# Long convolutions by FFT: 128x128 transpositions on TensorE instead of shuffles by DMA

## The chip, the cores and the metric

The kernel runs on one core of a Trainium2 chip. The metric is the time of one execution on the device in microseconds (us). Of the kernel before, three timed runs gave 4006.89, 4009.58 and 4015.99 us; their median is 4009.58 us.

## What is computed

The reference is a pair of transformer-like blocks, each a token mixer and a mixture of experts. The change touches the mixer of the first block alone, a Hyena operator on 1024 tokens of 1024 channels: two long convolutions, each gated, with filters as long as the sequence on both sides.

```python
def long_conv(zin, o):
    zf = zin.astype(F32)
    y = jnp.fft.irfft(jnp.fft.rfft(zf, n=2 * L, axis=1) * kf[None, :, o], n=2 * L, axis=1)[:, :L]
    return (y + zf * f_bias[o].astype(F32)).astype(h.dtype)
z = x1 * long_conv(v, 0)
z = x2 * long_conv(z, 1)
return z @ w_out + b_out
```

`L` is 1024, so the transforms have length 2048. `kf` are the spectra of the filters, which the kernel computes beforehand.

## The kernel before

The program runs in stages. First come the filters' spectra (`filters`), the input's norm and the input projection, woven together. Then comes `gamma`, all the long convolutions. After it `hyena_out` projects the result, and the experts, the second block and its experts follow. `gamma` is the stage of the change.

A transform of 2048 is done in two steps, over 128 x 16. A token is n = 16 n1 + n2. A stage of products over n1 turns 64 values of n1 (the other 64 are the zero padding) into 128 rows of sines and cosines; a second one, over n2 and a group of 8 rows, gives the spectrum, in 16 blocks. Between the two, what stood on partitions as (row of 8, block) with n2 along the free side must stand as (n2, row of 8) on partitions with the block along the free side. The inverse has the same two stages in reverse. All data are float32; a float32 product is two records of TensorE in the trace.

`convs` is one stream: two quarters of the channels (256 each), for each quarter both convolutions. Two streams run. For each convolution a stream does the following, and the shared pool `fft2` with five buffers of 128 x 16 x 256 (`shuf`) holds A, B, Y, C and E of both streams:

- *First stage* (L424): for each of 8 steps two products of 128 columns by 256, over all 128 partitions of `z`. Partitions 0 to 63 and 64 to 127 hold two different n2, so the table `f1z` has zeros for the half that is not meant. ScalarE copies the PSUM bank (tag `c1`, named `c` in the trace) to A (L425).
- *Shuffle* (L282, called for each n2): SyncE issues a DMA from A to B, 128 KB from all partitions to 8 partitions. 16 for a convolution.
- *Spectrum* (L292, `spectrum`): for each of 8 steps four 128 x 64 products by 256, of which two write partitions 0 to 63 and two 64 to 127. `consume` multiplies by the filter's spectrum, with VectorE (L437, L438), and adds up on VectorE and GpSimd (L448, L449) into Y.
- *Third stage* (L459): the inverse of the second, 16 products by 256, copied by ScalarE to C (L460); then 16 shuffles from C to E (L462).
- *Last stage* (L472): 16 products of 128 x 64 into tag `tp`; for the first convolution VectorE multiplies by the gate into `z` (L475), for the second ScalarE copies to `zt`, TensorE transposes (L485), VectorE multiplies by the gate (L487), and the result `zc` goes to DRAM.

The filter's spectra `kl`, the gate and the next `z` are loaded by SyncE too, so they stand in the same queue as the shuffles. PSUM has 3 banks of `c1`, 2 of `tp` and 3 of `ri`. Which stream's step is written next is set in `gamma` by a table `GP` of rests; the framework's scheduler then orders each engine's instructions by its own model.

Of the kernel before, what the change touches and what calls it, by code (L numbers as in the profile page):

```python
# [23 lines left out]
OP = mybir.AluOpType  # L24
# [14 lines left out]
def host_consts():  # L39
    """Tables that depend on shapes alone."""  # L40
# [23 lines left out]
    # by place in a block of 8, then block  # L64
# [37 lines left out]
    c["g2i"] = Gi.reshape(128, 2048)  # L102
# [25 lines left out]
    # t > j, t <= i, t < j, t >= i: in chunks of 64, then in one of 128  # L128
# [9 lines left out]
    # rows (segment, expert): same expert, and earlier segment of it  # L138
# [5 lines left out]
def bcast(ap, n, off=0, parts=128):  # L144
    """Row of a DRAM tensor on every partition."""
    return bass.AP(tensor=ap.tensor, offset=ap.offset + off, ap=[[0, parts], [1, n]])


def turn_pair(ap):
    """[p, 2, n] with the two swapped."""  # L150
    a = [list(x) for x in ap.ap]
    return bass.AP(tensor=ap.tensor, offset=ap.offset + a[-2][0], ap=[*a[:-2], [-a[-2][0], 2], a[-1]])


def turned(ap):
    """[..., n] with the last in reverse."""
# [4 lines left out]
def weave(*gens):  # L161
    """Emits generators in turn: (generator, yields, from, to) over a span of 1."""
# [8 lines left out]
def part(g, n):  # L171
    """The next n steps of a generator."""
# [4 lines left out]


GP = (1.0, 1.0, 0, 0, 8)


class Kern:
# [17 lines left out]
    def behind(self, *marks):  # L200
        """What is traced here is issued after these, engine by engine."""
# [10 lines left out]
    sep = "tp"  # tag of transposes  # L212
# [4 lines left out]
    # ------------------------------------------------------------------ hyena  # L217
    def hyena_tables(self, pool, inv):
# [4 lines left out]
        else:  # L223
            self.f1z = self.load(pool, "f1z", [128, 2, 128], I["k_f1z"].rearrange("p (h m) -> p h m", h=2))
# [72 lines left out]
    def filters(self, ctx):  # L297
        """Spectra of the two filters, normalised, with the bias as a tap at zero, to DRAM."""
# [26 lines left out]
        def taps(o, q):  # L325
# [4 lines left out]
            for n2 in range(16):  # L330
# [6 lines left out]
                # sum of the positive taps: with that of all taps, it gives the sum of their sizes  # L337
# [11 lines left out]
        def out(o, q, B, acc):  # L349
# [41 lines left out]
    def convs(self, i, qs, wk, wk2):  # L391
        """Both long convolutions of quarters of the channels, gated, tokens in (n2, n1) order: from xg[0]
        by tokens to zc by channels. A step is a bank of products; a shuffle follows steps 8 and 24 of the 32."""
        nc, CW = self.nc, self.CW
        own = lambda name, shape, p=wk: p.tile([128, *shape], F32, name=f"{name}{i}", bufs=1)
        shuf = lambda: self.fft.tile([128, 16, CW], F32, name="shuf")

# [21 lines left out]
        for n, (q, o) in enumerate([(q, o) for q in qs for o in range(2)]):  # L419
            A, B = shuf(), shuf()  # L420
            for j in range(8):
                pa = self.pt(self.ps, "c1", [2, CW])
                for h in range(2):
                    nc.tensor.matmul(pa[:, h, :], lhsT=self.f1z[:, h, :], rhs=z[:, j, :], start=(h == 0), stop=(h == 1), skip_group_check=True)  # L424
                nc.scalar.copy(A[:, 2 * j:2 * j + 2, :], pa)  # L425
                for h in range(2):
                    self.shuffle(A, B, 2 * j + h)
                if j == 7:
                    g = gates(o, q)
                yield  # L430
            Y = shuf()
# [1931 lines left out]
```

## Time and profile before

| what | value |
|---|---|
| median of 3 runs | 4009.58 us (4006.89 to 4015.99) |
| profiled execution, first to last instruction | 4012.2 us |
| TensorE busy, whole span | 3334.1 us (83%) |
| VectorE busy | 2680.1 us (67%) |
| ScalarE busy | 1914.8 us (48%) |
| GpSimd busy | 894.5 us (22%) |
| stage of the long convolutions | 678.3 to 1176 us |

The profiled execution's own time is the span; it lies among the times of the three runs. The stage is 12% of it. Busy times of TensorE count a product's whole passage through the array, so that neighbours overlap: the time from start to start is what a product costs in a row of products.

### The profile page before, as it was taken

To read this page: it belongs to the slowest core of one execution; us is meant where nothing else is said; L and a number is where in the kernel's file an instruction comes from. 1 tells how busy PE (TensorE), PEld (TensorE's weight loads), DVE (VectorE), ACT (ScalarE), POOL (GpSimd) and SP (SyncE) were. 2 spreads that over 40 slices of the span, in tenths; PEclk is the share of its full clock that TensorE was granted. 3 is DMA by queue.
4 is the path that set the end of the run, shared out by engine and by line. 5 is a ranking of instruction groups with operands and counts; after the bars stand their busy time and mean duration, and the time that the engine had idled before them with its cause. 6 is when DMAs were issued, how large, how long until landed. Compare 5 with 4: busy or idle time off the path is not lost. (4 is left out here: it accounts for less than half of the span.)

```text
span 4012.2 us, 48518 instructions
## 1 busy us (share of the span) xinstructions
PE 3334.1 (83%) x17602; PEld 2631.6 (66%) x17602; DVE 2680.1 (67%) x3397; ACT 1914.8 (48%) x2511; POOL 894.5 (22%) x829
## 2 busy tenths in 40 slices
PE   4699998455649699999999999779987898895996
PEld 2466666333337578877777777567877797783775
DVE  5443442432439778888888888767538886757987
ACT  5433332111124356666666666566424443333665
POOL 1111110221216501020001000020136444423331
PEclk8899999777879799999999999989998998896998
DMA  8667674776774699999999999746543435427998
GB/s 230 103 169 168 152 197 141 132 145 114 152 168 125 204 338 367 357 348 363 361 351 368 358 368 352 247 146 196 159 154 97 120 104 151 158 95 260 370 359 307
DMA packets 558959, 908.43 MB, mean 226 GB/s; under 512 B 88696, under 2 KB 291039, under 8 KB 555615
## 3 DMA queue, kind: packets, MB, share of 16 engines
q1 hardware_dynamic: 542608, 852.42, 68.0%
q0 software_dynamic: 11312, 43.26, 3.9%
q10 hardware_dynamic: 4800, 9.64, 0.7%
q8 instruction: 140, 2.29, 0.2%
q14 instruction: 99, 0.81, 0.1%
HBM read 735.40 MB, written 119.48 MB: 213 GB/s over the span
## 5 line engine op out<-in xcount | busy, mean ns | idle before, releaser
L518 DVE TENSOR_TENSOR wl<-raw,wh 128x2048 fp32r<-128x2048 f32 x474 | 1067.1, 2286 | 114.4 <-ACT wh L517 113.4
L517 ACT CAST wh<-raw 128x2048 fp32r<-128x2048 f32 x480 | 889.2, 1907 | 80.8 <-PE ab L526 36.9
L525 PE MATMUL ab<-wl,xT 128*128 128x512 f32 x1280 | 515.4, 403 | 37.4 <-DVE wl L518 37.4
L524 PE MATMUL ab<-wh,xT 128*128 128x512 f32 x1280 | 511.4, 402 | 1.1 <-ACT wh L517 1.1
L526 PE MATMUL ab<-wh,xT 128*128 128x512 f32 x1280 | 510.8, 399 | 0.0
L525 PEld LDWEIGHTS ab<-wl,xT 128*128 128x128 f32 x1280 | 243.7, 190 | 106.0 <-DVE wl L518 52.1
L524 PEld LDWEIGHTS ab<-wh,xT 128*128 128x128 f32 x1280 | 243.5, 190 | 59.0 <-ACT wh L517 3.3
L526 PEld LDWEIGHTS ab<-wh,xT 128*128 128x128 f32 x1280 | 243.1, 190 | 54.4
L525 PE MATMUL y<-wl,hT 128*128 128x512 f32 x640 | 257.0, 402 | 0.2 <-DVE wl L518 0.2
L292 PE MATMUL ri<-shuf,g2f 128*64 128x256 f32 x1024 | 154.5, 430 | 122.9 <-DMA shuf<-shuf 115.7
L1078 POOL DMA_INDIRECT xe<-hl,idx x32 | 52.2, 1631 | 908.1 <-DVE idx L1076 810.0
L524 PE MATMUL y<-wh,hT 128*128 128x512 f32 x640 | 253.1, 396 | 1.5 <-DVE ye L1157 1.5
L526 PE MATMUL y<-wh,hT 128*128 128x512 f32 x640 | 252.9, 395 | 0.0
L292 PEld LDWEIGHTS ri<-shuf,g2f 128*64 128x64 f32 x1024 | 77.3, 152 | 187.3 <-issue 133.1
L525 PE MATMUL u<-h2T,pwh 128*128 128x512 f32 (+1 forms) x400 | 161.1, 404 | 3.3 <-DVE h2T L518 3.3
L1166 POOL DMA_INDIRECT acc<-ye,idx x30 | 106.0, 3533 | 255.3 <-DVE ye L1157 221.8
L526 PE MATMUL u<-h2T,pwl 128*128 128x512 f32 (+1 forms) x400 | 160.6, 403 | 0.0
L517 ACT CAST hT<-tp 128x512 fp32r<-128x512 f32 x80 | 46.9, 586 | 235.8 <-PE tp L1109 235.8
L524 PE MATMUL u<-hT,uwh 128*128 128x512 f32 x384 | 158.5, 413 | 1.1 <-ACT ub L701 0.9
L524 PE MATMUL u<-h2T,pwh 128*128 128x512 f32 (+1 forms) x400 | 157.5, 402 | 0.0
L437 DVE TENSOR_TENSOR t<-ri,kl 128x512 f32<-128x512 f32 x64 | 43.9, 686 | 167.1 <-PE ri L292 89.1
L525 PE MATMUL u<-hT,uwh 128*128 128x512 f32 x384 | 155.3, 404 | 0.0
(548 smaller groups left out, 7196.5 us busy)
## 6 DMA issues: line engine op xcount, KB each, us to landing
raw<-in_moe_w_dram SPq DMA_DIRECT2D x384, 1024.0 KB
shuf<-shuf SPq DMA_DIRECT2D x384, 128.0 KB
raw<-in_exp_w_gate_dram SPq DMA_DIRECT2D x32, 1024.0 KB
raw<-in_exp_w_up_dram SPq DMA_DIRECT2D x32, 1024.0 KB
raw<-in_exp_w_down_dram SPq DMA_DIRECT2D x32, 1024.0 KB
pwl<-in_w_in_dram SPq DMA_DIRECT2D x37, 512.0 KB
gw<-in_mod_w_dram SPq DMA_DIRECT2D x32, 512.0 KB
kf<-kst SPq DMA_DIRECT2D x32, 512.0 KB
```

The costliest lines, as they stand in the source:

```text
L292: nc.tensor.matmul(ri[s * 64:s * 64 + 64, t, :], lhsT=self.g2f[:, 2 * qq + s, o:o + 64], rhs=B[:, 2 * qq + s, :], start=(t == 0), stop=(t ...
L437: nc.vector.tensor_tensor(t1[0][:, h], ri, k, op=OP.mult)
L517: c = self.nc.scalar.copy(hi, src)
L518: (eng or self.nc.vector).tensor_tensor(lo, src, hi, op=OP.subtract)
L524: nc.tensor.matmul(pt, lhsT=l[0], rhs=r[0], start=first, stop=False)
L525: nc.tensor.matmul(pt, lhsT=l[0], rhs=r[1], start=False, stop=False)
L526: nc.tensor.matmul(pt, lhsT=l[1], rhs=r[0], start=False, stop=last)
L1078: nc.gpsimd.indirect_dma_start(out=xe, out_offset=None, in_=hlD, in_offset=bass.IndirectOffsetOnAxis(ap=idx[:, 0:1], axis=0))
L1166: nc.gpsimd.indirect_dma_start(out=accD, out_offset=row, in_=ye, in_offset=None, compute_op=OP.add)
```

## The change

A and C are now made with the channels on partitions: the data `z` and Y are the stationary side of the product and the tables the moving one. A 128 x 128 transposition on TensorE for each block (or n2) and half of the channels then brings the rows back to partitions, and ScalarE or VectorE copies it out of PSUM to B or E. The first stage's table has no zeros any more: a product takes the 64 partitions of one n2 alone, the other half's product goes to another PSUM bank and another half of the array's rows. Its copies write runs of 8 elements into A. The third stage's products write PSUM in runs of 8 elements with gaps (`pa[:, c, :, s, :]`). The order of steps in `convs` changes: the transpositions of the next step are written before the spectrum products of this one, and the third stage's products inside the spectrum's loop, two steps behind. Two steps of the last stage share a bank of tag `ri` in place of one of `tp` each. The next `z` is loaded at the end of the second convolution's first stage. `GP` is gone: the streams are woven at an offset of half a convolution. Comments are gone in the whole file, so line numbers differ. The shuffles in `filters` stay.

```diff
-    fz = np.zeros((128, 2, 128))
-    fz[:64, 0] = F1t[:64]
-    fz[64:, 1] = F1t[:64]
-    c["f1z"] = fz.reshape(128, 256)
+    c["f1n"] = np.concatenate([F1[:64], F1[:64]])
...
-    c["g2i"] = Gi.reshape(128, 2048)
+    c["g2i"] = Gi.reshape(128, 16, 8, 16).transpose(0, 1, 3, 2).reshape(128, 2048)
...
-            A, B = shuf(), shuf()
-            for j in range(8):
-                pa = self.pt(self.ps, "c1", [2, CW])
+            A = shuf()
+            Av = chans(A)
+            for j, c in ((0, 0), (0, 1), (4, 0), (4, 1)):
+                pa = [self.pt(self.ps, "c1", [4, 128]) for _ in range(2)]
+                for m in range(4):
+                    for h in range(2):
+                        r = slice(h * 64, h * 64 + 64)
+                        nc.tensor.matmul(pa[h][:, m, :], lhsT=z[r, j + m, c * 128:c * 128 + 128], rhs=self.f1n[r, :],
+                                         start=(m == 0), stop=(m == 3), tile_position=(h * 64, 0), skip_group_check=True)
                 for h in range(2):
-                    nc.tensor.matmul(pa[:, h, :], lhsT=self.f1z[:, h, :], rhs=z[:, j, :], start=(h == 0), stop=(h == 1), skip_group_check=True)
-                nc.scalar.copy(A[:, 2 * j:2 * j + 2, :], pa)
-                for h in range(2):
-                    self.shuffle(A, B, 2 * j + h)
-                if j == 7:
+                    nc.scalar.copy(Av[:, c].rearrange("p b (n k) -> p n b k", k=8)[:, 2 * j + h:2 * j + h + 7:2], pa[h].rearrange("p n (b k) -> p n b k", k=8))
+                if j and c:
                     g = gates(o, q)
+                    if o == 1 and q != qs[-1]:
+                        z = first(qs[qs.index(q) + 1])
                 yield
-            Y = shuf()
+            B, Y = shuf(), shuf()
+            def turn(qq):
+                pt = self.pt(self.ps, "tp", [2, CW])
+                for s in range(2):
+                    for c in range(2):
+                        b = 2 * qq + s
+                        nc.tensor.transpose(pt[:, s, c * 128:c * 128 + 128], Av[:, c, b, :], self.ident)
+                nc.scalar.copy(B[:, 2 * qq:2 * qq + 2, :], pt)
...
-            yield from self.spectrum(B, consume)
-            C, E = shuf(), shuf()
-            for b in range(8):
-                pa = self.pt(self.ps, "c1", [2, CW])
-                for h in range(2):
-                    nc.tensor.matmul(pa[:, h, :], lhsT=self.g2i[:, 2 * b + h, :], rhs=Y[:, 2 * b + h, :], start=(h == 0), stop=(h == 1), skip_group_check=True)
-                nc.scalar.copy(C[:, 2 * b:2 * b + 2, :], pa)
-                for h in range(2):
-                    nc.sync.dma_start(E[16 * b + 8 * h:16 * b + 8 * h + 8], C[:, 2 * b + h, :])
+            def back(b):
+                if b == 0:
+                    C.append(shuf())
+                pa = self.pt(self.ps, "c1", [2, 16, 2, 8])
+                for s in range(2):
+                    for c in range(2):
+                        nc.tensor.matmul(pa[:, c, :, s, :], lhsT=Y[:, 2 * b + s, c * 128:c * 128 + 128], rhs=self.g2i[:, 2 * b + s, :],
+                                         start=(s == 0 and c == 0), stop=(s == 1 and c == 1), skip_group_check=True)
+                nc.scalar.copy(chans(C[0])[:, :, :, 16 * b:16 * b + 16], pa.rearrange("p c n s k -> p c n (s k)"))
+            C = []
+            sp = self.spectrum(B, consume)
+            turn(0)
+            for qq in range(8):
+                if qq < 7:
+                    turn(qq + 1)
+                next(sp)
+                if qq % 2 and qq > 1:
+                    back(qq - 3)
+                    back(qq - 2)
...
-            for j in range(8):
-                pa = self.pt(self.ps, "tp", [CW])
+            for j in range(0, 8, 2):
+                for k in (j, j + 1):
+                    pt = self.pt(self.ps, "tp", [2, CW])
+                    for h in range(2):
+                        for c in range(2):
+                            nc.tensor.transpose(pt[:, h, c * 128:c * 128 + 128], Cv[:, c, 2 * k + h, :], self.ident)
+                    if k % 2:
+                        nc.vector.tensor_copy(E[:, 2 * k:2 * k + 2, :], pt)
+                    else:
+                        nc.scalar.copy(E[:, 2 * k:2 * k + 2, :], pt)
+                pa = self.pt(self.ps, "ri", [2, CW])
...
+        weave(*[(self.convs(i, (i, i + 2), wk, wk2), 4 * 18 + 1, i * 9 / 81, (72 + i * 9) / 81) for i in range(2)])
```

First place: TensorE's order in the first stage of the second quarter's convolutions, before. L424 is the first stage, L472 the last stage, `c_...` the PSUM bank.

```order
L424 MATMUL c_5900<-z_5755,f1z 128x256 x2
L472 MATMUL tp<-shuf,if_5058 64x256 x4
L424 MATMUL c_5910<-z_5755,f1z 128x256 x2
L424 MATMUL c_5920<-z_5755,f1z 128x256 x2
L424 MATMUL c_5942<-z_5755,f1z 128x256 x2
L472 MATMUL tp<-shuf,if_5058 64x256 x4
```

The same place now. L427 is the first stage (two banks for the two halves), L443 the transposition to B, L288 the spectrum, L474 the third stage.

```order
L443 MATMUL tp<-ident,shuf 128x128 x4
L474 MATMUL c_6796<-g2i,shuf 128x16x8 x4
L427 MATMUL c_6802<-f1n,z_5588 128x128 x4
L288 MATMUL ri<-shuf,g2f 64x256 x4
L427 MATMUL c_6803<-f1n,z_5588 128x128 x4
L288 MATMUL ri<-shuf,g2f 64x256 x3
L427 MATMUL c_6829<-f1n,z_5588 128x128 x2
L427 MATMUL c_6830<-f1n,z_5588 128x128 x2
```

Two products of 256 columns a bank have become four of 128 columns a bank, and the two halves of a pair (c_6802 and c_6803) stand apart, with the other stream's spectrum between.

Second place: TensorE's order in the middle of a spectrum, before. L292 is the spectrum, L459 the third stage.

```order
L459 MATMUL c_5275<-shuf,g2i 128x256 x2
L292 MATMUL ri<-shuf,g2f 64x256 x8
L459 MATMUL c_5292<-shuf,g2i 128x256
L459 MATMUL c_5307<-shuf,g2i 128x256
L292 MATMUL ri<-shuf,g2f 64x256 x4
L459 MATMUL c_5292<-shuf,g2i 128x256
```

The same place now. L504 is the transposition to E, L512 the last stage of the other stream.

```order
L443 MATMUL tp<-ident,shuf 128x128 x4
L288 MATMUL ri<-shuf,g2f 64x256 x4
L504 MATMUL tp<-ident,shuf 128x128 x8
L512 MATMUL ri<-shuf,if_5178 64x256 x2
L443 MATMUL tp<-ident,shuf 128x128 x4
L288 MATMUL ri<-shuf,g2f 64x256 x4
L512 MATMUL ri<-shuf,if_5178 64x256 x2
L504 MATMUL tp<-ident,shuf 128x128 x8
L474 MATMUL c_7006<-g2i,shuf 128x16x8 x4
```

Each spectrum step now has its transpositions in front of it, and the other stream's last stage stands between them with its own.

Third place: SyncE's queue around the first spectra, before. `kl`, `gate` and `z` are loads, the two lines of `shuf<-shuf` in question are L282 and L462.

```order
L282 DMA shuf<-shuf 8x16x256 x2
L412 DMA gate_5189<-xg_72 128x8x256
L406 DMA kl_0_5313<-kf 128x2048
L462 DMA shuf<-shuf 8x16x256 x8
L406 DMA kl_0_5314<-kf 128x2048
L462 DMA shuf<-shuf 8x16x256 x4
L406 DMA kl_1_5410<-kf 128x2048
```

The same place now.

```order
L411 DMA gate_5283<-xg_72 128x8x256
L192 DMA if_5178<-in_k_if_dram 128x64
L405 DMA kl_0_5249<-kf 128x2048
L405 DMA kl_0_5250<-kf 128x2048
L405 DMA kl_1_5570<-kf 128x2048
```

The loads stand one behind the other, with no shuffle between.

## Rows read from the trace of the kernel before

**Rows 1.** Windows: each stretch with its length, busy time by engine, clock, DMA.
```profile
core 0: us, PE busy (x) PEld busy (x) DVE busy (x) ACT busy (x) POOL busy (x), PEclk, DMA share, GB/s
678.30:1176.00 497.70, 263.25 (x1344) 165.97 (x1344) 166.20 (x240) 86.07 (x162) 110.61 (x80) 0.76 0.72 137
...
1040.00:1100.00 60.00, 45.13 (x232) 26.84 (x231) 23.72 (x41) 13.74 (x24) 13.85 (x10) 0.88 0.65 155
```

**Rows 2.** Waits, 665 to 1180 us: engine, line, releaser, total us, times, longest.
```profile
PE ri L292 <- DMA shuf<-shuf: 97.5, 6, 29.4
...
PE tp L472 <- DMA shuf<-shuf: 89.0, 7, 21.8
...
PE tp L472 <- DMA ld<-in_hy_w_out_dram: 28.6, 1, 28.6
...
PE ri L292 <- DVE t L438: 5.7, 4, 3.2
```

**Rows 3.** DMA in the stage: queue (packets, MB, share), issues.
```profile
q1 hardware_dynamic: 47251, 67.81, 71.8%
...
shuf<-shuf SPq DMA_DIRECT2D x256, 128.0 KB
```

**Rows 4.** Timeline at the stage's end: start, length, instruction, idle time before and releaser.
```profile
1166.97 3.57 PE L472 MATMUL tp<-shuf,if 128*64 128x256 f32 x16 [28.61 <-DMA ld<-in_hy_w_out_dram]
...
1184.21 0.79 PE L524 MATMUL u<-Wo,zT 128*128 128x512 f32 x1 [6.51 <-DMA zr<-zc]
```

**Rows 5.** Timeline of TensorE in a dense stretch of a spectrum.
```profile
758.77 1.95 PE L292 MATMUL ri<-shuf,g2f 128*64 128x256 f32 x16
...
766.87 1.13 PE L459 MATMUL c<-shuf,g2i 128*128 128x256 f32 x4
...
767.93 1.08 PE L292 MATMUL ri<-shuf,g2f 128*64 128x256 f32 x8
...
768.95 1.99 PE L459 MATMUL c<-shuf,g2i 128*128 128x256 f32 x8
```

**Rows 6.** Timeline of TensorE: eight transpositions and what follows them.
```profile
907.57 1.04 PE L485 MATMUL tp<-ident,zt 128*128 128x128 f32 x8
908.45 1.03 PE L459 MATMUL c<-shuf,g2i 128*128 128x256 f32 x4
```

**Rows 7.** Timeline of TensorE in the delta rule: 128x128 products, then others.
```profile
3200.35 2.05 PE L1784 MATMUL g<-R,w 128*128 128x128 f32 x16 [0.17 <-DVE qT L1711]
3202.15 0.36 PE L1716 MATMUL g<-cmask,idr 128*128 128x256 f32 x1
```

**Rows 8.** Groups by line in the stage: busy us, mean ns, idle before.
```profile
L437 DVE TENSOR_TENSOR t<-ri,kl 128x512 f32<-128x512 f32 x64 | 43.9, 686 | 167.1 <-PE ri L292 89.1 <-issue 77.1
...
L425 ACT COPY shuf<-c 128x512 f32<-128x512 f32 x64 | 37.3, 586 | 113.7 <-PE c L424 89.0 <-DMA shuf<-shuf 24.7
...
L475 DVE TENSOR_TENSOR z<-tp,gate 128x256 f32<-128x256 f32 x32 | 13.6, 425 | 89.0 <-PE tp L472 87.7 <-PE ri L292 1.2
```

**Rows 9.** Groups by line, whole span: two ScalarE copies of one size.
```profile
L1400 ACT COPY pub<-u 128x512 f32<-128x512 f32 x18 | 18.9, 1061 | 2.7 <-PE u L526 2.7
...
L1459 ACT COPY pub<-u 128x512 f32<-128x512 f32 x14 | 8.2, 584 | 14.3 <-PE u L526 14.3
```

**Rows 10.** Windows of the delta rule, columns as in rows 1.
```profile
3060.00:3120.00 60.00, 52.09 (x411) 50.51 (x411) 48.89 (x123) 29.75 (x82) 30.23 (x32) 0.93 0.32 86
3120.00:3180.00 60.00, 49.60 (x397) 46.58 (x397) 53.65 (x113) 27.84 (x83) 31.21 (x37) 0.95 0.45 131
3180.00:3240.00 60.00, 54.79 (x434) 53.15 (x434) 51.66 (x123) 30.89 (x93) 27.81 (x32) 0.91 0.40 113
3240.00:3300.00 60.00, 55.09 (x467) 52.55 (x465) 48.13 (x131) 27.70 (x78) 18.85 (x23) 1.00 0.40 108
```

More of the change, by code (lines that the diff above doesn't have):

```diff
@@ L176, in part @@
         yield
-GP = (1.0, 1.0, 0, 0, 8)
 class Kern:
@@ L223, in hyena_tables @@
         else:
-            self.f1z = self.load(pool, "f1z", [128, 2, 128], I["k_f1z"].rearrange("p (h m) -> p h m", h=2))
+            self.f1n = self.load(pool, "f1n", [128, 128], I["k_f1n"])
             self.g2i = self.load(pool, "g2i", [128, 16, 128], I["k_g2i"].rearrange("p (b m) -> p b m", b=16))
@@ L396, in convs @@
         shuf = lambda: self.fft.tile([128, 16, CW], F32, name="shuf")
+        chans = lambda x: x.rearrange("p a b -> p (a b)").rearrange("p (c n k) -> p c n k", c=2, n=16)
         def first(q):
@@ L453, in convs @@
             t1 = []
-            yield from self.spectrum(B, consume)
-            C, E = shuf(), shuf()
-            for b in range(8):
-                pa = self.pt(self.ps, "c1", [2, CW])
-                for h in range(2):
-                    nc.tensor.matmul(pa[:, h, :], lhsT=self.g2i[:, 2 * b + h, :], rhs=Y[:, 2 * b + h, :], start=(h == 0), stop=(h == 1), skip_group_check=True)
-                nc.scalar.copy(C[:, 2 * b:2 * b + 2, :], pa)
-                for h in range(2):
-                    nc.sync.dma_start(E[16 * b + 8 * h:16 * b + 8 * h + 8], C[:, 2 * b + h, :])
-                if b == 7:
+            def back(b):
[17 more added lines that the diff above has]
+                    back(qq - 2)
+                if qq == 7:
+                    next(sp, None)
                     if o == 0:
@@ L466, in convs @@
                     elif q != qs[-1]:
-                        z, kl = first(qs[qs.index(q) + 1]), spectra(0, qs[qs.index(q) + 1])
+                        kl = spectra(0, qs[qs.index(q) + 1])
                 yield
-            for j in range(8):
-                pa = self.pt(self.ps, "tp", [CW])
-                for h in range(2):
-                    nc.tensor.matmul(pa[h * 64:h * 64 + 64, :], lhsT=self.if1, rhs=E[:, 2 * j + h, :], start=True, stop=True,
-                                     tile_position=(0, h * 64), skip_group_check=True)
+            for b in (6, 7):
+                back(b)
+                yield
+            E, Cv = shuf(), chans(C[0])
+            for j in range(0, 8, 2):
[9 more added lines that the diff above has]
+                pa = self.pt(self.ps, "ri", [2, CW])
+                for k in range(2):
+                    for h in range(2):
+                        nc.tensor.matmul(pa[h * 64:h * 64 + 64, k, :], lhsT=self.if1, rhs=E[:, 2 * (j + k) + h, :], start=(k == 0), stop=(k == 1),
+                                         tile_position=(0, h * 64), skip_group_check=True)
                 if o == 0:
-                    nc.vector.tensor_tensor(z[:, j, :], pa, g[:, j * CW:j * CW + CW], op=OP.mult)
+                    nc.vector.tensor_tensor(z[:, j:j + 2, :], pa, g[:, j * CW:j * CW + 2 * CW].rearrange("p (j c) -> p j c", j=2), op=OP.mult)
                     yield
@@ L479, in convs @@
                     zt = wk2.tile([128, 4, CW], F32, name="zt")
-                nc.scalar.copy(zt[:, j % 4, :], pa)
-                if j % 4 == 3:
+                nc.scalar.copy(zt[:, j % 4:j % 4 + 2, :], pa)
+                if j % 4 == 2:
                     for c in range(2):
@@ L487, in convs @@
                         nc.vector.tensor_tensor(gs, gs, pt, op=OP.mult)
-                if j == 7:
+                if j == 6:
                     nc.sync.dma_start(self.zc[q], g.rearrange("p (k t) -> p k t", k=2))
@@ L500, in gamma @@
         wk2 = ctx.enter_context(tc.tile_pool(name="cvx", bufs=2))
-        gens = [self.convs(i, (i, i + 2), wk, wk2) for i in range(2)]
-        steps = []
-        for i in range(2):
-            t = GP[4] * i
-            for n in range(4 * 32 + 1):
-                steps.append((t, i))
-                t += (GP[1], GP[0], GP[1], GP[1])[n // 8 % 4]
-                if n % 16 == 7:
-                    t += GP[3] if n % 32 == 7 else GP[2]
-        for _, i in sorted(steps):
-            next(gens[i], None)
+        weave(*[(self.convs(i, (i, i + 2), wk, wk2), 4 * 18 + 1, i * 9 / 81, (72 + i * 9) / 81) for i in range(2)])
     def split(self, hi, lo, src, eng=None):
```

## The prediction

> **What bounds the kernel now.** I read the windows first, because the diff touches one stage: the long convolutions between 678.3 and 1176 us. The reader is to see in [rows 1] that this stage takes 497.70 us and TensorE is busy for 263.25 of it, at a mean granted clock of 0.76. VectorE (166.20), GpSimd (110.61) and ScalarE (86.07) are idle for longer still. So no engine bounds the stage. The waits come next: in [rows 2] TensorE stands for 97.5 us in front of L292 and 89.0 us in front of L472 until a shuffle has landed, and 28.6 us until a load of `w_out` has. These three are 215.1 of TensorE's 234.45 idle microseconds. Waits for ScalarE and VectorE are some us each, of which 5.7 for L438. Then the DMA view: 256 shuffles of 128 KB, 33.5 of the stage's 67.81 MB, and a queue whose packets hold 71.8% of the sixteen engines [rows 3]. The timeline shows the last and dearest case: TensorE starts again at 1166.97 after 28.61 us, since the last four shuffles are followed in the same queue by six loads of `w_out` [rows 4]. The stage is therefore a chain of shuffles with idle engines. What follows starts when it ends: TensorE's first instruction of the output projection is at 1184.21, behind `zr`, a load of the stage's result [rows 4], so time saved in the stage moves everything behind it.
>
> **What goes.** All 256 shuffles of this stage, their waits (215 us of TensorE, with the `w_out` collision), and their place in SyncE's queue, where `kl`, `gate` and `z` now stand one behind the other (third place of the order). About 34 MB of loads and stores remain; over some 365 us that is 94 GB/s, less than the 137 that the stage moves now, so I give transfers no place on the path. The shuffles of the filter stage stay.
>
> **What comes, on TensorE.** The prices per product are start-to-start times at full clock. A 128x256 product of two records: x8 lasts 1.99 us and x4 1.13 us, so four records are 0.86 us and a product 0.43 us [rows 5]. A spectrum step (four 128x64 products, two at a time): x16 against x8, 1.95 less 1.08, 0.87 us [rows 5]. A change of the array's tile shape: from 766.87 to 767.93 are 1.06 us, 0.20 more than the 0.86 of work; from 767.93 to 768.95 are 1.02, 0.15 more than 0.87; I take 0.175 [rows 5]. A 128x128 transposition: eight between 907.57 and 908.45, 0.11 us [rows 6]. A 128x128 product with a stationary side of its own, which is what the first and the third stage become: 16 records between 3200.35 and 3202.15, two to a product, 0.225 us [rows 7].
>
> The stage before, at these prices: L424 and L459 128 products each, 55.0 us each; 64 spectrum steps 55.7; 32 like steps of L472 27.8; 64 transpositions 7.0; 136 changes of shape (counted in the order) 23.8; 224 us in all. The row says 263, so half-clock stretches cost about 39.
>
> The stage after: first stage 256 products of 128 columns, 57.6; transpositions there and back 512, 56.3; spectrum 55.7; third stage 256 products, 57.6; last stage 27.8; final transpositions 7.0; together 262.0. The pairs of 64-row products are meant to run side by side. But the order puts most of them four of one half, then four of the other (first place): only 59 neighbours in the whole stage are of different halves. If each overlapped wholly this would give 13 us back, if none nothing; I take 6. Changes of shape rise to 281 by the same count, 49.2 us. Sum 305 us of TensorE at full clock, against 224: the change adds 81 us of TensorE work, and the shuffles' waits are what pays for it.
>
> **What lies beside it.** ScalarE takes 64 copies after the transpositions and 32 more before the last stage, at 0.586 [rows 8]: 86 becomes about 140 us. The first stage's 64 copies now write runs of 8 elements. The nearest rows are 0.586 for a contiguous copy of this size [rows 8], 0.584 for another and 1.061 for one that writes single elements far apart [rows 9]; I take 0.586, and the other end adds 30 us to ScalarE. At 170 of 365 us it would still be hidden, except where TensorE waits for one of the three `c` banks.
> The Trainium skill, "SBUF — State Buffer" (Door 1: The DMA port swizzle, the note on cachelines), says that accesses in one 16-byte line run at full rate and a new line for each costs extra. By it 8 fp32 in a row fill two lines, the copy stays at 0.586, and [rows 9] show the other side of the rule; the sum is the same.
> VectorE takes 32 copies of 512 out of PSUM, bounded by 0.425 and 0.686 [rows 8]: 22 us at the dearer. Its 32 products for `z` become 16 of twice the size, 13.6 to about 11. It ends near 186 us; GpSimd stays at 111. Both are covered by TensorE's 305.
>
> **The wait that takes their place.** Every block goes TensorE, PSUM copy, TensorE. In the order a L512 mostly follows the L504 x8 whose copies it needs, or one short piece of the other stream (second place). A copy is 0.59 to 0.69 us, and behind the waiting product stand, in TensorE's queue, the other stream's transpositions and spectrum, and VectorE behind those. There are 32 such pairs, and 64 of L443 and L288. I price this by the nearest stretch that is such a ping-pong of 128x128 products and copies, the delta rule from 3060 to 3300 us: TensorE is busy 52.09, 49.60, 54.79 and 55.09 of 60 us each, 88%, at a clock of 0.95 in the mean [rows 10]. So 305 / 0.95 = 321 us busy, / 0.88 = 365 us for the stage, 133 less than 497.7.
>
> The profiled span is 4012.2 us, 2.6 above the median of the timed runs. 4012.2 - 132.7 = 3879.5, and as a median 3877 us. That is my forecast, with a range of its own of 3850 to 3903 (busy shares of 0.95 and 0.82).
>
> **Rivals.**
> *Interleaved PSUM writes are slow.* L474 writes its 128 columns as 16 runs of 8 floats with gaps. No row has such a write, so its price lies between 0.225 and any multiple; I take 0.225, for the same count of columns [rows 7]. At double, TensorE has 57.6 us more: (305 + 57.6) / 0.95 / 0.88 = 434, total 3946. Against it: runs of 8, not single elements.
> The Trainium skill, "PSUM — Partial Sum Buffer" (Specifications), speaks for it: PSUM has 8-byte lines, and "any non-contiguous AP slows matmuls significantly". Its reason, two floats to a line, speaks against it here.
> *The short chains decide.* TensorE is held as it is between 1040 and 1100 us, the best stretch of the stage now: 45.13 of 60 us, 75% [rows 1]. Then 321 / 0.75 = 428 us, total 3940. For it: five `shuf` buffers for two streams that each want up to four; against it: that stretch still holds shuffles.
> *Better than the delta rule.* All pairs run side by side (57.6 / 2 = 28.8 saved, 22.8 more than assumed), full clock, 95% busy: 282 / 0.95 = 297, total 3809. For it: nearly all idle time of today is DMA's. Against it: the order.
> *Slower.* The clock stays at 1.2 GHz: the work doubles to 610, / 0.88 = 693, total 4205. It decides once 305 has become 0.88 x 497.7 = 438, when 44% of the work runs at half clock. For it: clocks of 0.76 and 0.88 in [rows 1]; against it: there TensorE had waited long for shuffles, and the delta rule holds 0.91 to 1.00 [rows 10].
> *No change.* TensorE waits as long for the remaining loads (`kl`, 2 MB per convolution, one buffer) and the stage keeps its length: 4010. Against it: bytes halve.
>
> **How the numbers follow.** Forecast 0.55, slow writes 0.12, short chains 0.14, better 0.13, slower 0.03, no change 0.03. The range of 3812 to 3948 us takes in the forecast's own, both dearer cases and most of the cheaper one. Differences under 0.2% (8 us) cannot be told from none. Faster is the sum of the first four, 0.94; same 0.03; slower 0.03.
>
> **What would show it.** In the new profile: no `shuf<-shuf` issue behind 678 us; a stage of about 365 us with TensorE busy near 320 at a clock of 0.95; L474 and L427 records 0.11 us apart, or 0.22 if slow writes hold; L427 neighbours side by side only at some 59 places; waits of TensorE for ScalarE's `shuf` copies of about 40 us in sum; later stages of the same length. I would be wrong if TensorE were idle for a quarter of the stage, or if the granted clock stayed below 0.85.

## The result, and the profile after

The changed kernel takes 3843.29 us (median of four runs, 3839.17 to 3850.69). The kernel before, in four runs that include one more beside it on the same chip, takes 4012.78 us (4006.89 to 4040.33). The ratio is 0.9553, with a 95% interval of 0.9517 to 0.9589: 4.5% faster. The forecast was 3877 us, 33.7 too slow; the time lies in its range. The profiled execution has a span of 3844.5 us, and the views in this section are read from it.

The windows come first: the stage, then two stretches of 60 us from its middle, its end, and the gap up to the next stage.

```profile
core 0: us, PE busy (x) PEld busy (x) DVE busy (x) ACT busy (x) POOL busy (x), PEclk, DMA share, GB/s
673.16:1008.94 335.78, 309.28 (x2368) 219.98 (x2368) 189.09 (x255) 135.07 (x241) 112.28 (x80) 0.98 0.29 103
733.00:793.00 60.00, 58.40 (x467) 42.58 (x468) 35.22 (x48) 27.43 (x50) 22.07 (x16) 1.00 0.37 123
793.00:853.00 60.00, 54.50 (x406) 38.12 (x404) 34.85 (x48) 22.06 (x40) 20.01 (x15) 1.00 0.26 88
973.00:1008.94 35.94, 28.37 (x182) 18.14 (x180) 15.32 (x21) 11.05 (x19) 9.22 (x7) 0.91 0.34 133
1008.94:1017.60 8.66, 0.26 (x3) 0.14 (x2) 8.66 (x12) 7.36 (x9) 0.00 (x0) 0.64 0.64 223
```

Against [rows 1] the stage is 161.6 us shorter: 335.8 us from its first to its last TensorE instruction, and 497.4 before, between the same two instructions (678.3 to 1175.7). TensorE is busy 92% of it at a clock of 0.98, where it was 53% at 0.76. VectorE (189), ScalarE (135) and GpSimd (112) all end far below TensorE's 309. So the stage has changed its kind: a chain of transfers has become a row of TensorE work. Idle time is densest at the end, where only one stream is left (TensorE busy 28.37 of 35.94 us). Most of it lies elsewhere all the same: of 26.5 idle us the last stretch has 7.6, and the four stretches of 60 us from 733 to 973 us (58.40, 54.50, 55.29 and 56.10 us busy) have 15.7.

The span is 167.7 us shorter. The stage gives 161.6; it also starts 5.2 us earlier, and what follows it takes 2835.5 us in place of 2836.5. Nothing was given back later. The 5 us are not the change's: in the kernels below that leave the program ahead of the stage as it is, it starts anywhere between 666.6 and 680.0 us.

The waits of TensorE in the stage (672 to 1010 us), all above 0.6 us:

```profile
engine line waited for: us in total, times, longest us
PE c L427 <- issue: 9.1, 1, 9.1
PE c L474 <- DVE shuf L462: 8.7, 5, 2.8
PE ri L512 <- ACT shuf L508: 4.2, 16, 0.3
PE ri L512 <- DVE shuf L506: 4.1, 4, 1.4
PE ri L288 <- ACT shuf L444: 2.4, 5, 0.5
PE c L474 <- POOL shuf L462: 1.9, 3, 1.2
PE tp L443 <- DVE gate L527: 1.7, 3, 0.6
PE tp L525 <- ACT zt L520: 1.0, 3, 0.3
PE tp L504 <- ACT shuf L476: 0.7, 1, 0.7
...
```

No line names a DMA; in [rows 2] three lines with DMAs held 215.1 us. The first line here lies ahead of the stage's first product. The others, with three smaller ones, make up nearly all of the stage's 26.5 idle microseconds. The copies out of PSUM that were to be the new wait take 11.7 of them (L512 8.3, L288 2.4, L504 0.7, and 0.3 at L443); the sums into Y, which the third stage reads, 10.6 (L474).

The DMA view of the same stretch answers to [rows 3]:

```profile
q1 hardware_dynamic: 12496, 34.62, 28.8%
...
kl<-kf SPq DMA_DIRECT2D x14, 1024.0 KB
```

The largest entry is now the loads of the filter's spectra; the shuffles are gone. And a line of the timeline of TensorE after the stage answers to [rows 4]:

```profile
1017.60 0.79 PE L554 MATMUL u<-Wo,zT 128*128 128x512 f32 x1 [7.24 <-DMA zr<-zc]
```

The output projection still starts behind the load of the stage's result, with 7.24 us of idle time before it (6.51 in [rows 4]). The 28.6 us for `w_out`, which stood in the queue behind the last shuffles, are gone.

The prices of the new products are read in the timeline of TensorE (columns: start, length, instruction, count of records, idle time before):

```profile
691.80 1.95 PE L474 MATMUL c<-g2i,shuf 128*128 128x128 f32 x16
693.68 1.95 PE L288 MATMUL ri<-shuf,g2f 128*64 128x256 f32 x16
...
698.37 2.56 PE L427 MATMUL c<-f1n,z 64*128 64x128 f32 x28
700.86 2.05 PE L474 MATMUL c<-g2i,shuf 128*128 128x128 f32 x16
...
710.42 1.08 PE L288 MATMUL ri<-shuf,g2f 128*64 128x256 f32 x8 [0.51 <-ACT shuf L444]
711.44 1.09 PE L504 MATMUL tp<-ident,shuf 128*128 128x128 f32 x8
712.82 0.65 PE L512 MATMUL ri<-shuf,if 128*64 128x256 f32 x4 [0.29 <-ACT shuf L508]
```

From 691.80 to 693.68 are 1.88 us for sixteen records that write PSUM in runs of eight floats, a change of shape at their end included: 0.118 each, where [rows 7] have 0.113; had such writes cost double, these sixteen would take 3.6 us. A narrower window (693.64 to 693.69 us) gives the start of the sixteenth by itself:

```profile
693.48 0.28 PE L474 MATMUL c<-g2i,shuf 128*128 128x128 f32 x1
```

So fifteen records are 1.68 us, 0.112 each, and the step over the change of shape is 0.20: the change costs 0.09 us. It does so throughout the stage: where shapes change at full clock, the next record starts 0.20 us after a 128-column record in place of 0.11, and 0.31 after a pair of 128x64 products in place of 0.21.

From 698.37 to 700.86 are 2.49 us for 28 records of the 64-row products, 0.089 each: some run beside their neighbour. In the whole stage 99 of these 512 records start within 0.035 us of the one before. The two idle times show the new ping-pong: the wait for a copy of 0.59 us is 0.3 to 0.5 us, because the next four transpositions stand between.

Groups by line, for the copies (664 to 1017 us):

```profile
L444 ACT COPY shuf<-tp 128x512 f32<-128x512 f32 x64 | 36.7, 589 | 61.4 <-PE tp L443 61.3
L430 ACT COPY shuf<-c 128x512 f32<-128x512 f32 x64 | 36.0, 587 | 48.9 <-PE c L427 44.5 <-PE ri L512 4.3
...
L506 DVE COPY shuf<-tp 128x512 f32<-128x512 f32 x32 | 22.0, 686 | 18.1 <-PE tp L504 17.8
```

The copy that writes runs of eight elements (L430) takes 0.587 us, no more than the contiguous one beside it (0.589), and VectorE's copy is at the dearer bound of [rows 8].

### The profile page after: what moved, and what is told of

The parts are those of the page before. It is cut to its first block, busy times and chain, and to the rows that moved or that the text cites. A ratio compares the mean times of both kernels' runs of the same rounds, so it can differ in the third digit from the quotient of the medians.

```text
span 3844.5 us, 50115 instructions
## 1 busy us (share of the span) xinstructions
PE 3370.0 (88%) x18626; PEld 2679.8 (70%) x18626; DVE 2706.1 (70%) x3413; ACT 1963.7 (51%) x2590; POOL 889.3 (23%) x829
## 4 chain that ended last, share of the span: by engine, by line
PE 49%; DVE 13%; DMA 5%; issue 3%; ACT 2%; SPq 1%; POOL 1%; DVEq 0%; POOLq 0%; ACTq 0%
PE ab L555 7%; PE ab L556 7%; PE ab L554 7%; PE y L555 4%; PE y L554 3%; PE y L556 3%; PE u L555 3%; PE u L556 3%; PE u L554 3%; DVE wl L548 3%; PE g L1814 1%; PE tp L1139 1%; DVE fs L1787 1%; ACT wh L547 1%; DVE sx L967 1%
## 5 line engine op out<-in xcount | busy, mean ns | idle before, releaser
L288 PE MATMUL ri<-shuf,g2f 128*64 128x256 f32 x1024 | 144.5, 401 | 19.0 <-DMA shuf<-shuf 14.6
L556 PE MATMUL u<-hT,uwl 128*128 128x512 f32 x384 | 154.9, 403 | 0.0
L1196 POOL DMA_INDIRECT acc<-ye,idx x30 | 94.9, 3164 | 251.9 <-DVE ye L1187 176.3
L554 PEld LDWEIGHTS y<-wh,hT 128*128 128x128 f32 x640 | 120.5, 188 | 30.0 <-ACT fjunk L1205 1.9
```

The source lines that it names most:

```text
L288: nc.tensor.matmul(ri[s * 64:s * 64 + 64, t, :], lhsT=self.g2f[:, 2 * qq + s, o:o + 64], rhs=B[:, 2 * qq + s, :], start=(t == 0), stop=(t ...
L554: nc.tensor.matmul(pt, lhsT=l[0], rhs=r[0], start=first, stop=False)
L556: nc.tensor.matmul(pt, lhsT=l[1], rhs=r[0], start=False, stop=last)
L1196: nc.gpsimd.indirect_dma_start(out=accD, out_offset=row, in_=ye, in_offset=None, compute_op=OP.add)
```

## The experiments

Ten kernels were run. Ratios are to the kernel before, run beside them on the same chip, with 95% intervals; "stage" is always from the first to the last TensorE instruction of the long convolutions. Lines are those of each kernel's own file.

| run | median us | ratio | stage us |
|---|---|---|---|
| the change | 3843.3 | 0.9553 [0.9517, 0.9589] | 335.8 |
| e4: 256 transpositions twice | 3876.4 | 0.9644 [0.9611, 0.9678] | 360.8 |
| e1: no 64-row products | 3855.0 | 0.9601 [0.9567, 0.9636] | 335.9 |
| e8: spectrum steps in pairs | 3847.6 | 0.9568 [0.9522, 0.9614] | 331.7 |
| e2: inverse half by shuffles | 3974.1 | 0.9882 [0.9844, 0.9919] | 472.2 |
| e3: forward half by shuffles | 4051.4 | 1.0082 [1.0036, 1.0128] | 532.1 |
| e5: both by shuffles, new order | 4157.9 | 1.0361 [1.0290, 1.0432] | 601.5 |
| e10: before, two queues | 4057.5 | 1.0100 [1.0034, 1.0167] | 536.8 |
| e9: filter stage turned too | 3817.7 | 0.9488 [0.9427, 0.9548] | 335.8 |
| e12: filter shuffles by ScalarE | 3866.1 | 0.9597 [0.9561, 0.9632] | 335.6 |
| e11: e9 and e8 | 3819.5 | 0.9478 [0.9443, 0.9513] | 335.9 |

**Does TensorE bound the stage now?** Each of the 256 transpositions to B is issued twice.

```diff
-                        nc.tensor.transpose(pt[:, s, c * 128:c * 128 + 128], Av[:, c, b, :], self.ident)
+                        for _ in range(2):
+                            nc.tensor.transpose(pt[:, s, c * 128:c * 128 + 128], Av[:, c, b, :], self.ident)
```

> The changed kernel with every transposition before the spectrum done twice, 256 more of 0.11 us. Theory (TensorE's own work sets the stage, 309 of 335.8 us busy): 25 to 30 us more, about 3870 us. Rival (short chains over PSUM copies set it, TensorE has slack): less than 10 us more, under 3853.

Measured: 3876.4 us, the stage 25.0 us longer. The windows of the stage of that kernel:

```profile
674.60:1035.30 360.70, 337.96 (x2624) 250.00 (x2624) 188.53 (x255) 136.48 (x241) 112.61 (x80) 0.97 0.27 96
```

TensorE is busy 28.7 us longer, and 25.0 of them appear in the length. 256 transpositions at 0.11 make 28. So the work on TensorE is on the path nearly one for one. The added work stands ahead of the copies, so it would lengthen a chain through them too; that TensorE is the bound rests on its busy share of 92% as well. The time is 33 us longer, over the 25 to 30 expected, for what follows the stage was 10 us longer as well, for which the edit gives no reason; over all kernels here it varies from 2830 to 2846 us.

**What are the 64-row products worth?** All 128 rows, with a table half zero as before.

```diff
-    c["f1n"] = np.concatenate([F1[:64], F1[:64]])
+    fz = np.zeros((128, 2, 128))
+    fz[:64, 0] = F1[:64]
+    fz[64:, 1] = F1[:64]
...
-                        r = slice(h * 64, h * 64 + 64)
-                        nc.tensor.matmul(pa[h][:, m, :], lhsT=z[r, j + m, c * 128:c * 128 + 128], rhs=self.f1n[r, :],
-                                         start=(m == 0), stop=(m == 3), tile_position=(h * 64, 0), skip_group_check=True)
+                        nc.tensor.matmul(pa[h][:, m, :], lhsT=z[:, j + m, c * 128:c * 128 + 128], rhs=self.f1n[:, h, :],
+                                         start=(m == 0), stop=(m == 3), skip_group_check=True)
```

> The changed kernel with the first stage's products over all 128 rows and a table that is zero for the other half, so no two of them can run side by side. Theory (the shuffles' waits are what went; TensorE's own work now sets the stage): the order of the changed kernel has only 59 neighbours of different halves and pays changes of tile shape for them; 256 products at 0.225 us are 57.6 against 46.7 measured in the stage, about 10 us more, and 59 changes of shape at 0.175 us fewer, about 10 us less: 3843 us, within 10. Rival (the pairs carry a good part of the gain): up to half of 57.6 us comes back, 3865 to 3872.

The stage keeps its length, 335.9 us, so the pairs are worth nothing there. The group of the first stage's products in that kernel (busy us, mean ns), and the same group in the changed kernel:

```profile
L429 PE MATMUL c<-f1n,z 128*128 128x128 f32 x512 | 68.2, 285 | 9.1 <-issue 9.1
```

```profile
L427 PE MATMUL c<-f1n,z 64*128 64x128 f32 x512 | 58.6, 295 | 9.1 <-issue 9.1
```

And the window of the stage without pairs:

```profile
667.70:1003.60 335.90, 309.76 (x2368) 228.35 (x2368) 189.48 (x255) 135.28 (x241) 112.42 (x80) 0.98 0.29 103
```

TensorE's time in these products is 68.2 us, and 58.6 with pairs (the 46.7 of the expectation is not what the group shows), so the pairs save 9.6 us. But 64-row products are a tile shape of their own, and without them the stage has 222 changes of shape in place of 281. At the 0.09 us read above, the 59 changes take back 5.5. What is left is small: busy time multiplied by the granted clock of the stage (0.984 here, 0.979 with pairs) is 304.8 and 302.8 us, so the pairs are worth some 2 us of work, and the clocks hide them. The median is 12 us higher, 0.5%, just outside the 10 expected, with runs from 3842.9 to 3863.3 that overlap the change's; the profiled execution is the fastest of them, so its trace cannot show where the others lose the time.

**Do fewer changes of shape help?** Two steps of the spectrum are written together, which leaves 254 changes.

```diff
-            for qq in range(8):
-                if qq < 7:
-                    turn(qq + 1)
+            turn(1)
+            for qq in range(0, 8, 2):
+                if qq < 6:
+                    turn(qq + 2)
+                    turn(qq + 3)
                 next(sp)
+                next(sp)
...
```

> The changed kernel with the spectrum's steps written two at a time (two transposition steps, two spectrum steps, two third-stage steps), which leaves 254 changes of tile shape in TensorE's order in place of 281. Theory (TensorE's own work sets the stage, changes of shape included): 27 x 0.175 = 5 us less, 3838. Rival (chains over VectorE set it): VectorE gets its spectrum steps in bursts, 5 to 15 us more.

The stage was 4.1 us shorter, near the 5 expected, and the time (3847.6) cannot be told from the change's. The profiled execution is the fastest of six (3832.5). The last experiment repeats this edit.

**Which half of the shuffles held the time?** First the inverse half alone goes back to shuffles, with its own copy and the 128x256 products.

```diff
-                nc.scalar.copy(chans(C[0])[:, :, :, 16 * b:16 * b + 16], pa.rearrange("p c n s k -> p c n (s k)"))
...
+                nc.scalar.copy(C[0][:, 2 * b:2 * b + 2, :], pa)
+                for h in range(2):
+                    nc.sync.dma_start(C[1][16 * b + 8 * h:16 * b + 8 * h + 8], C[0][:, 2 * b + h, :])
```

> The changed kernel with the shuffles between third and last stage back as DMAs (128 of the 256), the forward ones by transposition, and the new order of steps. Theory: TensorE has about 45 us less to do (256 transpositions at 0.11, 93 changes of shape fewer), but 8 waits for 16 shuffles each come back; 215 us over 16 such waits are 13 us each, 107 us: 3890 to 3930 us. Rival (the new order of steps gave the gain, not the transpositions): within 20 us of 3843.

Then the forward half alone.

```diff
-                    nc.scalar.copy(Av[:, c].rearrange("p b (n k) -> p n b k", k=8)[:, 2 * j + h:2 * j + h + 7:2], pa[h].rearrange("p n (b k) -> p n b k", k=8))
...
+                nc.scalar.copy(A[:, 2 * j:2 * j + 2, :], pa)
+                for h in range(2):
+                    self.shuffle(A, B, 2 * j + h)
```

> The other half: the shuffles between first stage and spectrum as DMAs, the inverse ones by transposition, the new order of steps; the first stage is that of the kernel before. Theory: as for the inverse ones, 3890 to 3930 us, rather the upper end, since the spectrum cannot start before the last of 16 shuffles has landed. Rival (order of steps): within 20 us of 3843.

Both expectations missed, and far: 3974 and 4051 us, where 3890 to 3930 stood. The second is even slower than the kernel before, which has both halves as shuffles. The waits of TensorE in the first:

```profile
PE ri L503 <- DMA shuf<-shuf: 136.7, 7, 25.7
PE ri L503 <- DMA ld<-in_hy_w_out_dram: 30.0, 1, 30.0
```

and in the second:

```profile
PE ri L291 <- DMA shuf<-shuf: 179.4, 7, 33.1
PE ri L291 <- DMA if<-in_k_if_dram: 38.3, 1, 38.3
```

The expectation had halved the waits with the number of shuffles. They do not halve. A wait is there once for each convolution (seven times, and an eighth time put down to the load that stands behind the shuffles in the queue), it lasts about as long as sixteen shuffles need to pass, and half of the shuffles are still one passage for each convolution. The timeline of SyncE's queue in the second kernel shows one:

```profile
682.69 25.61 SPq L281 DMA_DIRECT2D shuf<-shuf x16
709.76 0.34 SPq L195 DMA_DIRECT2D if<-in_k_if_dram x1
```

Sixteen are issued over 25.6 us, 1.6 each, and the load of `if` goes out only behind them. The last of ScalarE's copies that feed them ends at 689.3 us, and an issue by itself takes 0.61; what SyncE stood for between the issues is not shown, but 2 MB of `kl` went out just ahead of them. In [rows 2] the kernel before had 13 waits for shuffles of 14.3 us each; here seven of 19.5 and 25.6.

**Is it the order of the steps?** Both halves as shuffles, in the new order: the two edits above together.

> All 256 shuffles as DMAs and the old first stage, but the new order of steps (third stage inside the spectrum's loop, streams half a convolution apart, no rests for shuffles). Theory (the transpositions are the gain; the new order alone does not help and has given up the rests that covered shuffles): if the two halves added up, the stage would be 472 + 532 - 336 = 668 us, 4180 us in all; at least slower than before, 4060 to 4190. Rival (the new order by itself is worth time and the two half experiments lost it to something else): faster than before, under 4000.

4157.9 us, 3.6% slower than before and inside the 4060 to 4190 expected. The four runs lie from 4116.0 to 4186.0, and the profiled one, with the stage at 601.5 us, is the fastest of them. The waits of TensorE:

```profile
PE ri L291 <- DMA shuf<-shuf: 258.4, 7, 47.3
PE ri L291 <- DMA if<-in_k_if_dram: 40.8, 1, 40.8
PE ri L493 <- DMA ld<-in_hy_w_out_dram: 25.4, 1, 25.4
...
```

and the window of the stage:

```profile
667.60:1269.10 601.50, 251.43 (x1344) 169.28 (x1344) 166.17 (x223) 85.02 (x147) 112.32 (x80) 0.70 0.59 113
```

With the same shuffles, the new order costs 104 us more than the old one (601.5 and 497.4). The new order leaves TensorE, which takes its products in order, standing in front of L291 until B is whole: 299.2 us there, against 97.5 in front of the spectrum's line in [rows 2]. It differs from the old one in several ways (the third stage inside the spectrum's loop, the offset of the streams, no rests); which of them costs the time was not tried. From this start the transpositions take off 265.7 us together; the forward ones alone 129 (e2), the inverse ones alone 69 (e3). So the half that goes first gains less than the one that goes last (136.4 from e2 to the change, 196.3 from e3). The transpositions in the old order were not tried, so what the order gives or takes once the shuffles are gone stays open.

**Was it only the queue?** The kernel before, with the inverse half's shuffles issued by ScalarE.

```diff
-                    nc.sync.dma_start(E[16 * b + 8 * h:16 * b + 8 * h + 8], C[:, 2 * b + h, :])
+                    nc.scalar.dma_start(E[16 * b + 8 * h:16 * b + 8 * h + 8], C[:, 2 * b + h, :])
```

> The kernel before with the 128 inverse shuffles issued by ScalarE in place of SyncE, so that they do not stand in one queue with the forward ones and the loads. Theory (a shuffle is dear because the DMA engines need about 1.5 us for its 128 KB, whichever queue it comes from): within 20 us of before. Rival (one queue, 0.61 us an issue, and what stands ahead in it, make the wait): 40 us or more less.

1% slower (4057.5, and 4017.1 before beside it): 40 us more, where one side expected no more than 20 either way and the other 40 less. The waits of ScalarE, then of TensorE:

```profile
ACT shuf L460 <- DMA shuf<-shuf: 213.0, 18, 43.7
...
PE ri L292 <- DMA shuf<-shuf: 114.3, 6, 30.3
PE tp L472 <- DMA shuf<-shuf: 53.3, 7, 12.5
PE c L459 <- ACT shuf L460: 29.1, 8, 9.1
```

TensorE's wait in front of L472 falls from 89.0 to 53.3 us, but ScalarE, which issues and copies PSUM, now stands itself for 213 us at this line (22.7 in the kernel before), and TensorE behind it for 29.1. A second queue moves the standing; it does not remove the passage.

**The same edit where shuffles seem covered.** The filter stage's 128 shuffles become transpositions too. The expectation was that this gives nothing, since TensorE has other work there.

```diff
-                pa = self.pt(ps, "c1", [CW])
-                nc.tensor.matmul(pa, lhsT=self.f1, rhs=hw, start=True, stop=True)
-                nc.scalar.copy(A[:, n2, :], pa)
-                self.shuffle(A, B, n2)
...
+                pa = self.pt(ps, "c1", [2, 128])
+                for c in range(2):
+                    nc.tensor.matmul(pa[:, c, :], lhsT=hw[:, c * 128:c * 128 + 128], rhs=self.f1, start=(c == 0), stop=(c == 1), skip_group_check=True)
+                nc.scalar.copy(Av[:, :, :, 8 * n2:8 * n2 + 8], pa.rearrange("p c (b k) -> p c b k", k=8))
...
+                        nc.tensor.transpose(pt[:, s, c * 128:c * 128 + 128], Av[:, c, 2 * qq + s, :], self.ident)
```

> The changed kernel with the filter stage's 128 shuffles replaced by 256 transpositions as well. Theory (a shuffle costs only where nothing else fills TensorE): there TensorE is busy 516 of 573 us and stands for shuffles about 15 us; 256 transpositions at 0.11 us, products in halves and some changes of shape are 30 to 40 us more, of which 15 come back: 3855 to 3870. Rival (any shuffle removed pays): 10 to 20 us less, under 3835.

The expectation fell: 3817.7 us, and the long convolutions start at 652.0 instead of 673.2 us. The windows of the filter stage in the changed kernel:

```profile
60.00:200.00 140.00, 89.51 (x441) 62.32 (x434) 69.35 (x160) 72.91 (x150) 13.96 (x19) 0.81 0.66 129
200.00:660.00 460.00, 445.19 (x2338) 314.03 (x2337) 197.63 (x314) 165.02 (x309) 64.59 (x150) 0.99 0.61 160
```

and in this one:

```profile
60.00:200.00 140.00, 124.71 (x768) 95.37 (x765) 83.54 (x180) 94.00 (x188) 19.25 (x31) 0.95 0.36 121
200.00:660.00 460.00, 441.57 (x2603) 325.28 (x2602) 187.44 (x296) 182.34 (x346) 60.02 (x139) 0.99 0.43 138
```

From 200 us on the expectation was right: TensorE is busy 96 to 97% of the time with shuffles and without. It was wrong for the first 140 us, where TensorE was busy 89.5 us and is now 124.7. The two largest waits of TensorE for transfers there in the changed kernel:

```profile
PE ri L288 <- DMA shuf<-shuf: 14.6, 1, 14.6
PE u L612 <- DMA upar_r<-in_hy_conv_b_dram: 10.1, 1, 10.1
```

Neither is left without the shuffles. The first, up to 104.12 us, is the passage of a set of sixteen. The second ends at 185.18 us, just ahead of the first product of the input projection (185.84): small loads had gone out behind shuffles, from 173.94 us on; they now go out from 139.75.

**Queue or passage in the filter stage?** The changed kernel, its 128 filter shuffles issued by ScalarE.

```diff
-        self.nc.sync.dma_start(B[8 * n2:8 * n2 + 8], A[:, n2, :])
+        self.nc.scalar.dma_start(B[8 * n2:8 * n2 + 8], A[:, n2, :])
```

> The changed kernel, in which ScalarE issues the 128 shuffles of the filter stage in place of SyncE; they stay shuffles. Theory 1, the place in SyncE's queue is what costs in the filter stage (TensorE stood 10.1 us for upar_r and 9.1 us for gw, loads issued behind shuffles): with the loads free, most of the 21 us that the transpositions gave come back, the long convolutions start near 655 us and the time is below 3832. Theory 2, the passage of a set of 16 shuffles is what costs (14.6 us of TensorE in front of L288, and an issue time of 1 to 2 us each): moving the issue only moves the standing to ScalarE, which copies PSUM and makes the filters' windows; the time is 3843 or more, up to 3890, and ScalarE shows waits for shuffles.

3866.1 us: SyncE's queue alone is not the cause. Three lines of TensorE's waits from 60 to 220 us and from 200 to 690 us:

```profile
PE u L612 <- DMA uraw<-in_hy_w_in_dram: 10.1, 1, 10.1
PE ri L288 <- DMA shuf<-shuf: 3.5, 1, 3.5
...
PE c L590 <- DMA gw<-in_mod_w_dram: 16.4, 4, 8.3
```

The wait in front of L288 shrinks, the 10.1 us at L612 stay, for another load now, and those for `gw` grow (9.1 in the changed kernel). ScalarE stands for shuffles for only 18.5 us, so the second theory has its time right and its reason not shown. The long convolutions now start 17 us later (690.4). Of this TensorE's waits give part: some 15 us more for loads of `gw` (from `mod_w` and `ada_w`), some 10 more for copies by ScalarE and windows by VectorE in the filters (L340), 11 less at L288. The rest is open.

**The two together.** The filters' transpositions and the spectrum's steps in pairs.

> The filter stage's transpositions and the spectrum's steps in pairs, both over the changed kernel. The two edits lie in different stages, and the stage that follows starts when the one before ends, so each should keep what it gave alone: the filters start the long convolutions 21 us earlier (652.0 instead of 673.2 us), the pairs took 4.1 us off the long convolutions' 335.8. Theory: the stage takes 331 to 333 us, and the time is 3811 to 3816, 2 to 6 us below the filters' edit alone (3817.7). Rival: a shorter stage is lost in the spread of the first loads (the stage has started between 652 and 680 us in kernels that differ only behind it): then the time is 3816 or more.

3819.5 us, the rival's side. The filters' gain is there again (the stage starts at 652.5 us; ratio 0.9478, its interval wholly below the change's). The pairs' 4.1 us are not: the stage takes 335.9 us. The windows of the stage in e8 and in this kernel:

```profile
669.10:1000.80 331.70, 306.54 (x2368) 220.84 (x2368) 185.53 (x255) 135.50 (x241) 112.19 (x80) 0.98 0.30 104
652.50:988.50 336.00, 310.17 (x2368) 224.54 (x2368) 185.89 (x255) 135.81 (x241) 112.25 (x80) 0.97 0.29 103
```

The work that the pairs save is there in both: busy time multiplied by the granted clock (0.979 and 0.967) is 300 us in e8 and in this kernel, and 302.8 in the change, 0.1 us for each of the 27 changes of shape. What this kernel lost is clock: it was granted the lower level, 1.2 GHz, for 22 us of the stage, and e8 for 14, most of the difference near the end (0.76 from 942.5 to 978.5 us, and 0.86 in e8's 36 us from 959.1, as far into its stage). Whether that comes of the order or of chance is not shown: there is one trace of each. The two versions with the filters' edit cannot be told apart; they are the best found, some 0.7% under the change.

## Why the prediction was right, step by step

- *What goes.* Right. The 215 us of waits for transfers in the stage are gone without a new one, and the rest of the program kept its length. It gave the new order no price of its own; with shuffles that order costs 104 us (e5), and with one half left as shuffles the kernel is 1.2% faster (e2) or 0.8% slower (e3) than before.
- *The work on TensorE, 305 us at full clock.* Right to 1%: 309.3 us busy at a clock of 0.979, which is 302.8 at full clock. e4 and the busy share of 92% say that it is this sum that sets the length. That the sum came out so near is in part luck, for two of its terms were off against each other. A change of shape was priced at 0.175 us, from stretches of [rows 5] that also hold short pauses within a group, and costs 0.09: 281 make 26 us, not 49.2. The products themselves took some 276 in place of 256: within a group a transposition starts 0.126 us after the last in the mean, not 0.11. The pairs were priced at 6 us and gave 9.6.
- *The copies.* ScalarE was forecast at 140 us and had 135.1, VectorE 186 and 189.1, GpSimd 111 and 112.3. Runs of eight elements cost nothing extra.
- *The wait that takes their place.* This is the mis-sized term. "305 / 0.95 = 321 us busy, / 0.88 = 365 us for the stage" priced idle time and clock by the delta rule [rows 10]. Measured are 309.3 and 335.8. Of the 29 us between 365 and 335.8, 12 are busy time (321 against 309.3, of which 9 are the clock) and 17 are idle time: 44 us were expected, most of it for copies out of PSUM, and 26.5 are there, 11.7 of them for those copies. Another 10.6 are the wait for the sums into Y, which the prediction had as covered. From 733 to 973 us TensorE is busy 56.1 of 60 us in the mean, 93%, and in the delta rule 88%. The next transpositions of the same stream and the products of the other stand between a copy and the product that needs it, so the sixteen waits at L512 for ScalarE are 0.3 us at most. How much of this the second stream gives is not shown: one stream alone keeps TensorE busy 22.33 of 23.44 us before the other's first product (696.6 us), and 28.37 of 35.94 at the end. That the delta rule lacks a second stream was not tried.
- *The remaining 6 us* of the 35 between the forecast's span and the measured one are the earlier start (5.2) and the rest of the program (1.0).
- *The rivals.* Slow interleaved writes: refuted by 0.118 us for each record, a change of shape included. The Trainium skill, "PSUM — Partial Sum Buffer" (Specifications), says that "any non-contiguous AP slows matmuls significantly"; for runs of eight floats the trace does not agree. Short chains: refuted by the busy share of 92%. Better than the delta rule: right on the clock, half right on the busy share, and too high on the pairs, of which it took all to run side by side: 99 records started beside the one before, where all pairs would be 256. Half clock and no change: refuted by 0.98 and by the empty DMA lines.

## What to carry to other kernels

Here a set of transfers between two dependent steps cost an engine that works in order one passage for each exposed place, not a price for each transfer: with half of the shuffles left, most of the waits stayed, and the half removed last gave the most. Before such a step is called covered, look at each stretch of its stage apart: the filters were covered for 460 us and bare in the first 140. An idle share is better borrowed from a stretch with as many independent streams, though that was not tried here. And a gain of a few microseconds inside a stage should be seen twice, and split into work, clock and idle time, before it is called kept or lost.

## What was not expected of the hardware

- The stage's 256 products of 64 rows, some of them side by side, took 9.6 us less than 256 of 128 rows, and a change between tile shapes cost 0.09 us, so the 59 that they add took 5.5 back.
- With 512 transpositions, woven with the other products in pieces of some 1 to 2 us, the granted clock of the stage was 0.98, where the stage with shuffles had 0.76, and 0.70 to 0.79 in the kernels that kept some.
- In e3 a set of sixteen shuffles of 128 KB, from all partitions to eight each, took 25.6 us to issue, though one issue takes 0.61, and a load of 32 KB went out only behind them.
